# Expert routing with one-hot products of nine columns, and gathered rows scaled on the ScalarE before a plain transpose

## The chip, the core and the metric

One core of a Trainium2 chip runs one layer of a network. The metric is the device time of one launch, in microseconds (us), as the median of a few runs. TensorE (PE in the profile, with its weight loads as PEld) multiplies matrices, VectorE (DVE) and ScalarE (ACT) work on elements, GpSimd (POOL) issues the transfers whose addresses are read from a tile, and SyncE (SP) issues the others.

## What is computed

The layer is attention and a short convolution, followed by a mixture of 16 experts, in which each expert chooses 128 of the 1024 tokens. The change lies in the second part:

```python
def ec_moe(x_tok, w_router, w_gate, w_up, w_down):
    cap = CAP_FACTOR * t // N_EXPERTS            # 128 tokens for each expert
    aff = jax.nn.softmax(logits, axis=-1)
    g, idx = lax.top_k(jnp.swapaxes(aff, 1, 2), cap)
    xs = jax.vmap(lambda xt, ix: xt[ix])(x_tok, idx)
    hg = jnp.einsum('becd,edf->becf', xs, w_gate)
    hu = jnp.einsum('becd,edf->becf', xs, w_up)
    y = jnp.einsum('becf,efd->becd', jax.nn.silu(hg) * hu, w_down) * g[..., None]
    # y is added into the rows idx of a zero array
```

`x_tok` is the RMS norm of the stream `h`, scaled and shifted. The kernel gathers rows of `h` itself and multiplies each by its own norm factor (1 over its root mean square) afterwards.

## The kernel before

The experts run one after the other, in the loop that begins at L1550. An expert's weights are 24 pieces of 512 KB, `raw`, loaded by SP into a ring of 30 pages; SP waits for a page to come free before it issues the next load. Each piece is split into two parts: ACT writes the high part `whi` (L157), DVE subtracts it and writes the low part `wlo` (L158). There are four buffers of each (`NSP = 4`), so ACT can be at most four pieces ahead of PE. PE uses a piece in six matmuls of 512 columns, in three kinds in turn: `whi` with the high part of the activations (L162), `wlo` with it (L163), `whi` with their low part (L164). In the order of pieces an expert has 4 for `hg`, 4 for `hu`, 4 for the second half of `hg`, 4 for the second half of `hu`, and 8 for the output `pyy`. This text counts them 1 to 24.

What the next expert needs is made by `route(e + 1)`, called after the first `hg`:

- DVE compares positions with a row of numbers and gets eight one-hot matrices `oh` (L1460).
- 24 small bf16 matmuls (L1465) multiply them with `tokb` into `pi`, three columns: the token's index, its gate and its norm factor. Each of the three is kept in three bf16 parts, which is why there are 8 times 3 matmuls: the parts are added in PSUM.
- ACT turns column 0 into the integer `idx` (L1467), and POOL issues the gather `xs <- hS` (L1469).
- DVE copies `pi` to `slot` (L1472) and makes `dgx`, the identity times the norm factor (L1474).

`xsplit`, called after the second `hu`, multiplies the gathered rows with `dgx` (L1511), which transposes and scales them at once, into `ptt`. ACT applies the affine (`xsy`, L1513), and ACT and DVE split it (`xsh`, `xsl`). At an expert's end ACT scales `pyy` by the gate into `y` (L1604) and POOL adds `y` into `ffS` by an indirect transfer (L1605).

SP's order is written by hand. The order on the other engines in this stage is made by a scheduler when the program is built, and each engine then runs its instructions in that fixed order.

Of the kernel before, what the change touches and what calls it, by code (L numbers as in the profile page):

```python
# [10 lines left out]
F32 = mybir.dt.float32  # L11
# [3 lines left out]
AF = mybir.ActivationFunctionType  # L15
OP = mybir.AluOpType
AX = mybir.AxisListType
# [3 lines left out]
P = 128  # L21
# [5 lines left out]
E = 16  # L27
KT = 8
# [119 lines left out]
def build(tc, nc, I, out, dbg=None):  # L148
    V, S, G, PE, SY = nc.vector, nc.scalar, nc.gpsimd, nc.tensor, nc.sync
# [3 lines left out]
    def f(ap):  # L153
        return ap.bitcast(F32)

    def split(hi, lo, src, eng=V):
        i = S.activation(hi, src, AF.Copy)  # L157
        eng.tensor_sub(lo, src, f(hi))  # L158
        return i
# [7 lines left out]
    with es:  # L167
# [4 lines left out]
        sm = es.enter_context(tc.tile_pool(name="sm", bufs=4))  # L172
        dr = es.enter_context(tc.tile_pool(name="dr", bufs=1, space=DRAM))
        pgA = es.enter_context(tc.tile_pool(name="pgA", bufs=NPA))
        psB = es.enter_context(tc.tile_pool(name="psB", bufs=3, space=PSUM))

        def pool(stack, name, bufs=1, **kw):
            return stack.enter_context(tc.tile_pool(name=name, bufs=bufs, reuse_waits="tile", **kw))

        def page(p, name, dt=F32, shape=(P, D)):  # L180
            return p.tile(list(shape), dt, name=name, tag="pg")

        def bank(shape, name):
            return psB.tile(list(shape), F32, name=name, tag="b")
# [42 lines left out]
        def const(n, shape, dt=F32, eng=SY):  # L227
            t = cp.tile(shape, dt, name=n)
            eng.dma_start(out=t, in_=I[n])
            return t  # L230
# [173 lines left out]
        for i, o in enumerate(ORDER.split()):  # L404
            if i == NL0:
                npm = const("npm", [P, KT])
                ident = const("ident", [P, P])
# [100 lines left out]
        for i in range(10):  # L508
# [6 lines left out]
            for j in range(2):  # L515
                S.dma_start(out=vS[:, :, j, i, :].rearrange("h p e -> p h e"),
                            in_=f(hl[:, j, :]).rearrange("p (h e) -> p h e", h=H))
# [632 lines left out]
        def transp(c, qt, g):  # L1150
            par = qt % 2
            k0, n = GRP[g]
            if par == 0:
                at[g] = (atp.tile([P, n, 2 * P], F32R, name=f"ath{g}"), atp.tile([P, n, 2 * P], F32R, name=f"atl{g}"))
            hi, lo = at[g]
            ps = psE[0].tile([P, 4, P], F32, name="ptr", tag="acc") if psE else bank([P, 4, P], "ptr")
            for j in range(n):
                PE.transpose(out=ps[:, j, :], in_=c[1][0][:, (k0 + j) * P:(k0 + j + 1) * P], identity=ident)  # L1158
            sl = slice(par * P, par * P + P)
            return hi[:, :, sl], lo[:, :, sl], ps[:, :n, :]  # L1160
# [84 lines left out]
        for i, (h, qt) in enumerate(seq):  # L1245
            j = i + 2
# [14 lines left out]
            def score():  # L1261
                c = scores(qq[j], KK[seq[j][0]])
                cs.append(c)
                return c
# [8 lines left out]
            c = None  # L1273
            if SO[i // 16] == 0:
                if j < N:
                    c = score()
                x0 = transp(cs[i], qt, 0)
                x1 = transp(cs[i], qt, 1)
# [15 lines left out]
            else:  # L1294
# [4 lines left out]
                if j < N:  # L1299
                    c = score()  # L1300
# [56 lines left out]
        def eacc(name):  # L1357
            return psE[0].tile([P, 512], F32, name=name, tag="acc")
# [22 lines left out]
        x1 = pool(e6, "x1")  # L1381
        tokb = rq.tile([P, KT, E, 3, 3], BF, name="tokb")
# [60 lines left out]
        pp = bank([P, KT, 2 * E], "pp5")  # L1443
# [5 lines left out]
        for j in range(KT - 1):  # L1449
            n = KT - 1 - j  # L1450
            PE.matmul(pp[:, j + 1:KT, :], onesb, gf[:, j:j + 1, :].to_broadcast([P, n, 2 * E]), start=False,
                      stop=(j == KT - 2))
# [5 lines left out]
        def route(e):  # L1458
            oh = x1.tile([P, KT, P], BF, name="oh")
            V.tensor_tensor(out=oh, in0=late["iota"][:, None, :].to_broadcast([P, KT, P]),  # L1460
                            in1=pos[:, :, e:e + 1].to_broadcast([P, KT, P]), op=OP.is_equal)
            pi = bank([P, 3], "pi")
            for j in range(KT):
                for k in range(3):
                    PE.matmul(pi, oh[:, j, :], tokb[:, j, e, k, :], start=(j + k == 0), stop=(j == KT - 1 and k == 2))  # L1465
            idx = sm.tile([P, 1], I32, name="idx")
            S.activation(idx, pi[:, 0:1], AF.Copy)  # L1467
            xs = x1.tile([P, D], F32, name="xs")
            G.indirect_dma_start(out=xs, out_offset=None, in_=hS[:, :],  # L1469
                                 in_offset=bass.IndirectOffsetOnAxis(ap=idx[:, :1], axis=0))  # L1470
            s = sm.tile([P, 3], F32, name="slot")
            V.tensor_copy(out=s, in_=pi)  # L1472
            dg = x1.tile([P, P], F32, name="dgx")
            V.tensor_scalar(dg, ident, s[:, 2:3], None, op0=OP.mult)  # L1474
            g = s[:, 1:2]
            return idx, g, xs, s, dg

        def tsplit(src, k0, hi, lo):
            pp = bank([P, 4, P], "ptt")
# [21 lines left out]
                hi, lo = w[kt // 2]  # L1501
                mm3(ps, xh_[:, kt, :], xl_[:, kt, :], hi[:, kt % 2, :], lo[:, kt % 2, :], kt == 0, kt == KT - 1)

        def xsplit(xs, dg, eng=V):

            hi, lo = x1.tile([P, KT, P], F32R, name="xsh"), x1.tile([P, KT, P], F32R, name="xsl")
            for k in range(0, KT, 4):
                pp = bank([P, 4, P], "ptt")
                y = x1.tile([P, 4, P], F32, name="xsy", bufs=2)
                for j in range(4):  # L1510
                    PE.matmul(pp[:, j, :], xs[:, (k + j) * P:(k + j + 1) * P], dg, start=True, stop=True)  # L1511
                for j in range(4):
                    S.activation(y[:, j, :], pp[:, j, :], AF.Identity, bias=mv[:, 1, k + j:k + j + 1],  # L1513
                                 scale=mv[:, 2, k + j:k + j + 1])
                split(hi[:, k:k + 4, :], lo[:, k:k + 4, :], y, eng)
            return hi, lo
# [22 lines left out]
        def glu(hg, hu):  # L1539
# [3 lines left out]
            return a  # L1543

        cur = route(0)
        first = chunk(0, 0)
        xh_, xl_ = xsplit(cur[2], cur[4], V)
        eD.close()
        e5.close()
        for e in range(E):  # L1550
            idx, g = cur[:2]
            ach, acl = x1.tile([P, KT, P], F32R, name="ach"), x1.tile([P, KT, P], F32R, name="acl")
            acts = []
            for fh in range(2):
                hg = eacc("hg")
                prod(hg, xh_, xl_, chunk(e, 2 * fh) if e or fh else first)
                if fh and e + 1 == E:
                    tcopy(acts[0], 0, ach)
                elif fh:
                    tsplit(acts[0], 0, ach, acl)  # L1560
                elif e + 1 < E:
                    nxt = route(e + 1)
                else:
                    bc["G2"] = page(pgA, "bcG2")
                    load_bc("G2")

                    ffg = page(pgA, "ffg")
                    G.indirect_dma_start(out=ffg, out_offset=None, in_=ffS[:, :],
                                         in_offset=bass.IndirectOffsetOnAxis(ap=idx[:, :1], axis=0))
                    for t in range(KT):  # L1570
                        fr.append(page(pgA, "ffr"))
                        G.dma_start(out=fr[t], in_=ffS[t * P:(t + 1) * P, :])
                hu = eacc("hu")
                prod(hu, xh_, xl_, chunk(e, 2 * fh + 1))
                acts.append(glu(hg, hu))
            if e + 1 < E:
                xh_, xl_ = xsplit(nxt[2], nxt[4])
            pys = [eacc("pyy") for _ in range(2)]
            if e + 1 == E:

                for i in range(KT):
                    if i == TSJ:
                        tcopy(acts[1], 4, ach)
                    if i % 2 == 0:
                        final(i // 2)
                    if not raws:
                        load_raw(pgX if (nraw[0] - NR0) % (NPA + NPX) < NPX else pgA)
                    raw = raws.popleft()
                    for dh in range(2):
                        PE.matmul(pys[dh], f(ach[:, i, :]), raw[:, dh, :], start=i == 0, stop=i == KT - 1)  # L1590
                continue
            for c in range(2):
                w = chunk(e, 4 + c)
                for j in range(4):
                    if c == 0 and j == TSJ:
                        tsplit(acts[1], 4, ach, acl)
                    hi, lo = w[j]
                    kt = 4 * c + j
                    for dh in range(2):
                        mm3(pys[dh], ach[:, kt, :], acl[:, kt, :], hi[:, dh, :], lo[:, dh, :], kt == 0, kt == KT - 1)  # L1600
            if e + 1 < E:
                y = x1.tile([P, D], F32, name="y")
                for dh in range(2):
                    S.activation(y[:, dh * 512:dh * 512 + 512], pys[dh], AF.Copy, scale=g[:, 0:1])  # L1604
                G.indirect_dma_start(out=ffS[:, :], out_offset=bass.IndirectOffsetOnAxis(ap=idx[:, :1], axis=0),  # L1605
                                     in_=y, in_offset=None, compute_op=OP.add)
                cur = nxt

        sl2 = sm.tile([P, 2], F32, name="ssl")
        for dh, sl in enumerate(halves):  # L1610
# [7 lines left out]
                             in_=ffg, in_offset=None)  # L1618
# [15 lines left out]
```

## Time and profile before

| what | value |
|---|---|
| median of 3 runs | 1348.53 us (1345.4 to 1351.03) |
| the profiled execution's own time | 1347.07 us |
| its span, first to last instruction | 1345.3 us |
| busy: PE, PEld | 92%, 75% of the span |
| busy: DVE, ACT | 80%, 59% |
| mean granted TensorE clock | 0.955 of full |
| the stage of the experts | about 735 to 1310 us |

A busy share is the time in which an engine executes something, over the span. It is a mean over stages with different limits, so the stage of the experts is read by itself further on.

### The profile page before, as it was taken

What the parts mean: (1) busy time and instruction counts of PE and PEld (TensorE: products, weight loads), DVE (VectorE), ACT (ScalarE), POOL (GpSimd) and SP (SyncE); (2) the same over time, 40 slices, a digit from 0 to 9 for tenths busy, and PEclk for the clock granted to TensorE, in tenths of its full rate; (3) what the DMA queues carried; (4) which work ended last, traced back from release to release, by engine and by line L of the source; (5) the groups of instructions that cost most, each with busy time, mean ns of one, the idle gap of its engine ahead of it and who ended that gap; (6) DMA issues with size and microseconds to landing.
All of it is one profiled execution on the core that took longest, in us unless ns stands there. A gap on an engine that the chain in (4) does not pass through costs nothing. (4 is left out here: it accounts for less than half of the span.)

```text
span 1345.3 us, 18451 instructions
## 1 busy us (share of the span) xinstructions
PE 1239.2 (92%) x6407; PEld 1009.8 (75%) x6407; DVE 1078.0 (80%) x1834; ACT 795.1 (59%) x1183; POOL 68.1 (5%) x64
## 2 busy tenths in 40 slices
PE   6999999999999799899863999999999999999993
PEld 2588887888888678677753888888888888877761
DVE  5972565979788857698867899999999999888865
ACT  5732112444344535454442988888888888887861
POOL 0000000000000000000000000000000000010022
PEclk8999999999999889899975999999999999999997
DMA  8449448355476963324197999999999999999497
GB/s 346 141 82 340 137 134 274 121 160 174 133 179 209 279 207 113 139 87 144 53 397 271 309 390 381 378 377 375 379 372 375 381 371 376 378 354 368 121 379 155
DMA packets 139053, 347.69 MB, mean 258 GB/s; under 512 B 16976, under 2 KB 59472, under 8 KB 138320
## 3 DMA queue, kind: packets, MB, share of 16 engines
q1 hardware_dynamic: 109760, 306.14, 63.9%
q0 software_dynamic: 7056, 25.69, 7.2%
q10 hardware_dynamic: 22144, 14.68, 3.8%
q8 instruction: 50, 0.82, 0.2%
q14 instruction: 43, 0.35, 0.1%
HBM read 297.17 MB, written 49.30 MB: 258 GB/s over the span
## 5 line engine op out<-in xcount | busy, mean ns | idle before, releaser
L158 DVE TENSOR_TENSOR wlo<-raw,whi 128x1024 fp32r<-128x1024 f32 x376 | 440.7, 1219 | 33.0 <-ACT whi L157 28.2
L157 ACT ACTIVATE whi<-raw 128x1024 fp32r<-128x1024 f32 x376 | 388.9, 1067 | 61.4 <-PE hu L164 27.9
L1131 ACT ACTIVATE e<-ps,nm 128x1280 f32<-128x1280 f32 x64 | 84.5, 1326 | 68.4 <-DVE nm L1127 52.8
L1127 DVE TENSOR_REDUCE nm<-ps 128x1 f32<-128x1280 f32 x64 | 92.5, 1482 | 17.5 <-PE ps L1118 17.4
L162 PE MATMUL hu<-whi,xsh 128*128 128x512 f32 x256 | 102.6, 401 | 1.6 <-ACT whi L157 1.6
L163 PE MATMUL hu<-wlo,xsh 128*128 128x512 f32 x256 | 101.8, 398 | 0.8 <-DVE wlo L158 0.8
L164 PE MATMUL hg<-whi,xsl 128*128 128x512 f32 x256 | 99.8, 390 | 1.1 <-DVE xsl L158 1.1
L163 PE MATMUL hg<-wlo,xsh 128*128 128x512 f32 x256 | 100.4, 392 | 0.0
L164 PE MATMUL hu<-whi,xsl 128*128 128x512 f32 x256 | 100.3, 392 | 0.0
L162 PE MATMUL hg<-whi,xsh 128*128 128x512 f32 x256 | 100.0, 390 | 0.0
L163 PE MATMUL pyy<-wlo,ach 128*128 128x512 f32 x240 | 94.9, 395 | 1.4 <-DVE wlo L158 0.9
L1118 PE MATMUL ps<-KK,q 128*128 128x512 f32 (+1 forms) x384 | 90.5, 382 | 6.1 <-ACT e L1131 3.6
L1163 ACT ACTIVATE ath<-ptr 128x512 fp32r<-128x512 f32 (+1 forms) x96 | 47.4, 525 | 80.9 <-PE ptr L1158 80.4
L162 PE MATMUL pyy<-whi,ach 128*128 128x512 f32 x240 | 94.1, 402 | 0.0
L164 PE MATMUL pyy<-whi,acl 128*128 128x512 f32 x240 | 93.9, 391 | 0.0
L1118 PEld LDWEIGHTS ps<-KK,q 128*128 128x128 f32 x384 | 64.8, 201 | 17.3 <-ACT e L1131 5.4
L671 PE MATMUL pf<-xh,wh 128*128 128x512 f32 x192 | 75.3, 392 | 1.7 <-DVE gc L689 1.7
L675 PE MATMUL pf<-xh,wl 128*128 128x512 f32 x192 | 75.9, 395 | 0.0
L673 PE MATMUL pf<-xl,wh 128*128 128x512 f32 x192 | 75.3, 392 | 0.0
L1166 DVE TENSOR_TENSOR atl<-ptr,ath 128x512 fp32r<-128x512 f32 (+1 forms) x96 | 55.5, 594 | 13.3 <-ACT ath L1163 13.0
L162 PEld LDWEIGHTS hu<-whi,xsh 128*128 128x128 f32 x256 | 48.4, 189 | 11.4 <-ACT whi L157 2.1
L163 PEld LDWEIGHTS hu<-wlo,xsh 128*128 128x128 f32 x256 | 48.6, 190 | 11.0 <-DVE wlo L158 1.8
(316 smaller groups left out, 2662.0 us busy)
## 6 DMA issues: line engine op xcount, KB each, us to landing
raw<-in_we SPq DMA_DIRECT2D x384, 512.0 KB, 9.5
wa<-in_wa SPq DMA_DIRECT2D x32, 512.0 KB, 5.8
wraw<-in_wF SPq DMA_DIRECT2D x20, 512.0 KB, 5.4
waw<-in_wa SPq DMA_DIRECT2D x16, 512.0 KB, 6.2
q<-qS SPq DMA_DIRECT2D x64, 128.0 KB, 4.8
mS<-hl SPq DMA_DIRECT2D x48, 128.0 KB, 4.7
vS<-hv ACTq DMA_DIRECT2D x20, 256.0 KB, 5.2
KK<-kS SPq DMA_DIRECT2D x16, 320.0 KB, 7.4
```

Of the source, the lines that this page charges most:

```text
L157: i = S.activation(hi, src, AF.Copy)
L158: eng.tensor_sub(lo, src, f(hi))
L162: PE.matmul(ps, wh, mh, start=first, stop=False)
L163: PE.matmul(ps, wh, ml, start=False, stop=False)
L164: PE.matmul(ps, wl, mh, start=False, stop=last)
L671: PE.matmul(ps, wh[:, kt, :], xh[kt][:, sl], start=first, stop=False)
L673: PE.matmul(ps, wh[:, kt, :], xl[kt][:, sl], start=False, stop=False)
L675: PE.matmul(ps, wl[:, kt, :], xh[kt][:, sl], start=False, stop=last)
L1118: PE.matmul(ps[:, m, k0:k0 + n], q[:, m, j, :], KK[:, m, k0:k0 + n], start=(j == 0), stop=(j == 1))
L1127: V.tensor_reduce(out=c[1][-1], in_=c[0][:, m, :], axis=AX.X, op=OP.max, negate=True)
L1131: S.activation(e, c[0][:, m, :], AF.Exp, bias=c[1][3 + m], accum_out=l[:, m:m + 1])
L1166: V.tensor_sub(x[1], x[2], f(x[0]))
```

## The change

The 24 small products become 8 of nine columns each, one for each block of 128 tokens; the three parts that PSUM used to add are added by a DVE reduction, which writes `slot`. `idx` is then a DVE copy from `slot` in place of an ACT instruction from `pi`. The matrix `dgx` goes. The gathered rows are scaled by an ACT instruction of 128x1024 (in place, except for the last expert), and transposed by PE against the plain identity.

```diff
-            pi = bank([P, 3], "pi")
+            pi = bank([P, 9], "pi")
             for j in range(KT):
-                for k in range(3):
-                    PE.matmul(pi, oh[:, j, :], tokb[:, j, e, k, :], start=(j + k == 0), stop=(j == KT - 1 and k == 2))
+                PE.matmul(pi, oh[:, j, :], tokb[:, j, e, :, :].rearrange("p k c -> p (k c)"), start=(j == 0),
+                          stop=(j == KT - 1))
+            s = sm.tile([P, 3], F32, name="slot")
+            V.tensor_reduce(out=s, in_=pi.rearrange("p (k c) -> p c k", c=3), axis=AX.X, op=OP.add)
             idx = sm.tile([P, 1], I32, name="idx")
-            S.activation(idx, pi[:, 0:1], AF.Copy)
+            V.tensor_copy(out=idx, in_=s[:, 0:1])
             xs = x1.tile([P, D], F32, name="xs")
             G.indirect_dma_start(out=xs, out_offset=None, in_=hS[:, :],
                                  in_offset=bass.IndirectOffsetOnAxis(ap=idx[:, :1], axis=0))
-            s = sm.tile([P, 3], F32, name="slot")
-            V.tensor_copy(out=s, in_=pi)
-            dg = x1.tile([P, P], F32, name="dgx")
-            V.tensor_scalar(dg, ident, s[:, 2:3], None, op0=OP.mult)
-            g = s[:, 1:2]
-            return idx, g, xs, s, dg
+
+            xn = xs if e + 1 < E else page(pgA, "xn")
+            S.activation(xn, xs, AF.Copy, scale=s[:, 2:3])
+            return idx, s[:, 1:2], xs, s, xn
...
-                    PE.matmul(pp[:, j, :], xs[:, (k + j) * P:(k + j + 1) * P], dg, start=True, stop=True)
+                    PE.transpose(out=pp[:, j, :], in_=xs[:, (k + j) * P:(k + j + 1) * P], identity=ident)
```

The scheduler moves things on three engines. On DVE, in each of the middle experts, the program before has this, from the split of the gathered rows on (`act` is the product of the two halves of the SwiGLU):

```order
L158 TENSOR_TENSOR xsl<-xsy,xsh 128x512
L158 TENSOR_TENSOR wlo<-raw,whi 128x1024 x11
L1460 TENSOR_TENSOR oh<-iota,pos 128x1024
L1472 COPY slot<-pi 128x3
L158 TENSOR_TENSOR wlo<-raw,whi 128x1024
L1474 TENSOR_SCALAR dgx<-ident,slot 128x128
```

The changed program has this at the same place:

```order
L158 TENSOR_TENSOR xsl<-xsy,xsh 128x512
L158 TENSOR_TENSOR wlo<-raw,whi 128x1024 x7
L1467 TENSOR_REDUCE slot<-pi 128x3
L1460 TENSOR_TENSOR oh<-iota,pos 128x1024
L158 TENSOR_TENSOR wlo<-raw,whi 128x1024
L1469 CAST idx<-slot 128x1
L158 TENSOR_TENSOR wlo<-raw,whi 128x1024 x6
L1542 TENSOR_TENSOR act<-act,hu 128x512
```

`slot` comes four pieces earlier, and `idx` follows it on DVE behind the next expert's `oh` and one more `wlo`: it stands right after the `wlo` of piece 4.

On ACT the program before has this from the output of the expert before on:

```order
L1604 ACTIVATE y<-pyy,slot 128x512 x2
L157 ACTIVATE whi<-raw 128x1024 x5
L1467 ACTIVATE idx<-pi 128x1
L1541 ACTIVATE act<-hg 128x512
L157 ACTIVATE whi<-raw 128x1024 x8
L157 ACTIVATE ach<-ptt 128x512
```

The changed program has this, here with the semaphores that each row waits for (DMASW is that of a POOL transfer, here the gather; DMAHW are those of the weight loads):

```order
L1604 ACTIVATE y<-pyy,slot 128x512 [waits PE_49] x2
L157 ACTIVATE whi<-raw 128x1024 [waits DMAHW6_49,DVE_49]
L157 ACTIVATE whi<-raw 128x1024 [waits DMAHW7_49,DVE_49,PE_49]
L157 ACTIVATE whi<-raw 128x1024 [waits DMAHW0_49,DVE_49,PE_49]
L157 ACTIVATE whi<-raw 128x1024 [waits DMAHW1_49,DVE_49,PE_49]
L157 ACTIVATE whi<-raw 128x1024 [waits DMAHW2_49,DVE_49,PE_49]
L1541 ACTIVATE act<-hg 128x512
L157 ACTIVATE whi<-raw 128x1024 [waits DMAHW3_49,DVE_49,PE_49]
L1475 ACTIVATE xs<-xs,slot 128x1024 [waits DMASW3_49]
L157 ACTIVATE whi<-raw 128x1024 [waits DMAHW4_49,DVE_49,PE_49]
L157 ACTIVATE whi<-raw 128x1024 [waits DMAHW5_49,DVE_49,PE_49]
```

`idx` is gone from ACT, and the scaling stands between the `whi` of piece 9 and that of piece 10. So five pieces lie between `idx` on DVE and the scaling on ACT. That holds for 9 of the gathers (for the experts of index 2 to 10); for the next two it is four pieces, and for the last three it is three. On PE the small products of the middle experts stand before among the matmuls of the same expert, between the first `hg` and `hu`; in the changed program they stand 26 matmuls into `pyy` of the expert before.

## Rows read from the trace of the kernel before

**Rows 1.** Windows of the experts' stage: busy us of each engine, granted clock, DMA.

```profile
core 0: us, PE busy (x) PEld busy (x) DVE busy (x) ACT busy (x) POOL busy (x), PEclk, DMA share, GB/s
735.00:1180.00 445.00, 445.00 (x2354) 369.97 (x2355) 404.88 (x405) 388.73 (x502) 39.39 (x25) 1.00 1.01 372
```

**Rows 2.** Waits of PE, 730 to 1310 us, the first of four: us, times, longest.

```profile
PE hu L162 <- ACT whi L157: 1.6, 1, 1.6
...
```

**Rows 3.** Timeline of PE: start us, us, what.

```profile
847.92 0.76 PE L1465 MATMUL pi<-tokb,oh 128*128 128x3 bf16 x24
848.54 0.47 PE L162 MATMUL hu<-whi,xsh 128*128 128x512 f32 x1
...
865.44 1.95 PE L1511 MATMUL ptt<-dgx,xs 128*128 128x128 f32 x16
867.14 0.48 PE L162 MATMUL pyy<-whi,ach 128*128 128x512 f32 x1
...
868.61 0.60 PE L1481 MATMUL ptt<-ident,act 128*128 128x128 f32 x4
868.96 0.48 PE L162 MATMUL pyy<-whi,ach 128*128 128x512 f32 x1
```

**Rows 4.** Timeline of ACT in the same expert, with idle before and its releaser.

```profile
849.08 0.15 ACT L1467 ACTIVATE idx<-pi 128x1 int32<-128x1 f32 x1
850.21 1.06 ACT L157 ACTIVATE whi<-raw 128x1024 fp32r<-128x1024 f32 x1 [0.49 <-PE hu L164]
851.57 1.06 ACT L157 ACTIVATE whi<-raw 128x1024 fp32r<-128x1024 f32 x1 [0.30 <-PE hu L164]
```

**Rows 5.** Timeline of DVE in the same expert.

```profile
835.83 8.04 DVE L158 TENSOR_TENSOR wlo<-raw,whi 128x1024 fp32r<-128x1024 f32 x7 [0.18 <-ACT whi L157]
849.05 1.22 DVE L1460 TENSOR_TENSOR oh<-iota,pos 128x1024 bf16<-128x1024 f32 x1
850.19 0.15 DVE L1472 COPY slot<-pi 128x3 f32<-128x3 f32 x1
```

**Rows 6.** Timeline of POOL in the same expert.

```profile
843.80 1.59 POOL L1605 DMA_INDIRECT ffS<-y,idx  x1 [28.86 <-ACT y L1604]
849.50 1.63 POOL L1469 DMA_INDIRECT xs<-hS,idx  x1 [4.10 <-ACT idx L1467]
```

**Rows 7.** DMA issues from 740 to 1180 us, median us from issue to landing.

```profile
ffS<-y,idx POOLq DMA_INDIRECT x12, 10.1
xs<-hS,idx POOLq DMA_INDIRECT x12, 8.2
```

**Rows 8.** Tile `xs`, 690 us to the end, all 16 gathers: time to landing.

```profile
DMA to landing us min/median/max: 5.2/8.2/11.8
```

**Rows 9.** Groups of ACT and DVE, 740 to 1180 us: busy us, mean ns | idle before.

```profile
L157 ACT ACTIVATE whi<-raw 128x1024 fp32r<-128x1024 f32 x293 | 304.8, 1068 | 54.2 <-PE hu L164 26.1 <-PE hg L164 19.7 <-PE pyy L164 6.0
L1604 ACT ACTIVATE y<-pyy,slot 128x512 f32<-128x512 f32 x24 | 15.0, 675 | 0.0
L158 DVE TENSOR_TENSOR wlo<-raw,whi 128x1024 fp32r<-128x1024 f32 x292 | 342.3, 1219 | 16.1 <-ACT whi L157 11.4
```

**Rows 10.** Timelines of ACT and PE in the last expert, 1286 to 1292 us.

```profile
1287.18 0.60 ACT L1541 ACTIVATE act<-hg 128x512 f32<-128x512 f32 x1 [3.18 <-PE hg L164]
...
1288.77 0.50 PE L162 MATMUL hu<-whi,xsh 128*128 128x512 f32 x1 [1.63 <-ACT whi L157]
1290.03 0.79 PE L163 MATMUL hu<-wlo,xsh 128*128 128x512 f32 x1 [0.76 <-DVE wlo L158]
```

**Rows 11.** Window of that place: the columns of rows 1.

```profile
1290.00:1293.40 3.40, 3.37 (x8) 2.68 (x9) 3.38 (x3) 2.39 (x3) 0.69 (x1) 0.53 1.02 374
```

**Rows 12.** DMA rate in 40 slices, 740 to 1180 us.

```profile
GB/s 276 379 269 356 412 406 325 414 404 339 379 410 352 367 410 356 351 414 403 330 406 407 335 368 410 359 354 409 406 324 415 403 325 385 409 360 359 411 366 347
```

**Rows 13.** Timelines of PE and ACT at the first gather.

```profile
728.66 3.76 PE L1511 MATMUL ptt<-dgx,xs 128*128 128x128 f32 x16 [5.83 <-DMA xs<-hS,idx]
730.74 1.51 ACT L1513 ACTIVATE xsy<-ptt,mv 128x128 f32<-128x128 f32 x4 [7.70 <-PE ptt L1511]
```

More of the change, by code (lines that the diff above doesn't have):

```diff
@@ L1502, in prod, with xsplit @@
                 mm3(ps, xh_[:, kt, :], xl_[:, kt, :], hi[:, kt % 2, :], lo[:, kt % 2, :], kt == 0, kt == KT - 1)
-        def xsplit(xs, dg, eng=V):
+        def xsplit(xs, eng=V):
             hi, lo = x1.tile([P, KT, P], F32R, name="xsh"), x1.tile([P, KT, P], F32R, name="xsl")
@@ L1546, in build @@
         first = chunk(0, 0)
-        xh_, xl_ = xsplit(cur[2], cur[4], V)
+        xh_, xl_ = xsplit(cur[4], V)
         eD.close()
@@ L1576, in build @@
             if e + 1 < E:
-                xh_, xl_ = xsplit(nxt[2], nxt[4])
+                xh_, xl_ = xsplit(nxt[4])
             pys = [eacc("pyy") for _ in range(2)]
```

## The prediction

> **What bounds the kernel now.** I read the windows first. From 735 to 1180 us PE is busy in all of the 445 us at the full granted clock, DVE in 404.88 and ACT in 388.73 [rows 1]. The waits of PE agree: from 730 to 1310 us they are of four kinds, the longest single one 1.6 us [rows 2]. So PE sets the pace of the middle experts, and DVE, at 91%, is close behind. The transfers are not the bound: SP's weight loads wait for free pages, and the rate reaches 415 GB/s in single slices against a mean of 372 [rows 1, 12]. Then I went through one expert engine by engine in the timelines [rows 3 to 6]. Two consecutive `whi`, each waiting for PE to free a buffer, start 1.36 us apart: that is PE's time for one piece of weights [rows 4]. ACT is thus held back to four pieces ahead of PE; DVE runs seven `wlo` on end behind ACT [rows 5]. An engine in front of PE that stops for long therefore starves PE after some three pieces, about 4 us. [...]
>
> **What the change takes from PE.** The 24 small products hold PE from 847.92 to 848.54, 0.62 us; eight cost a third, 0.21, if each matmul costs the same with nine columns as with three [rows 3]. The 16 passes of the product with `dgx` (two records for each matmul) hold it from 865.44 to 867.14, 1.70 us. Four plain transposes hold it from 868.61 to 868.96, 0.35, so eight cost 0.70 [rows 3]. That is 0.41 + 1.00 = 1.41 us for an expert, all on the path as long as PE is the bound. For 15 experts: **-21.0 us**.
>
> **DVE and ACT by volume.** DVE loses `dgx` and a copy and gets a reduction and a copy of one column; nothing of weight. ACT gets 1.07 us for each expert, by the `whi` of the same shape [rows 9], less the 0.15 of `idx` [rows 4]. By two `y` of half the size it would be 1.35 [rows 9]. ACT's 388.73 of 445 us [rows 1] become about 0.9 of the time: by volume this is hidden behind PE.
>
> **The wait that the change adds.** The scaling stands in ACT's order between the `whi` of pieces 9 and 10, and it waits for the gather. Behind it are queued all further `whi`, and behind them `wlo` and PE. The gather can't be issued before `idx`, which now stands on DVE. I put it together on the clock of the expert in the rows:
>
> - The seven `wlo` end at 835.83 + 8.04 = 843.87 [rows 5]. The chain from `ptt` over `xsy` to these is held by ACT and DVE, so I leave it where it is.
> - Reduction 0.2 (the copy of the same three columns takes 0.15; the reduction of nine is not in this trace), `oh` 1.22, `wlo` 1.22, `idx` 0.15: 846.7 [rows 5, 9].
> - POOL starts 0.27 us after `idx` is done, as before [rows 4, 6]: 846.9. It is free then, its scatter having taken from 843.80 to 845.39 [rows 6].
> - The gather takes 8.2 us from issue to landing [rows 7]: 855.1.
> - Scaling 1.07, `whi` of piece 10 1.06, its `wlo` 1.22: **858.5** [rows 4, 9].
>
> PE needs that `wlo` for the second matmul of piece 10. Before, `hu` begins at 848.54; five pieces and one matmul later (5 x 1.36 + 0.23, and 0.08 for the slower first step) it is 855.65. In the changed kernel PE is there 1.41 us sooner: **854.2**. So PE is late by 4.3 us, three times the 1.41 that it gains (each PE wait then is a little under that, since the first `oh` of the list already holds up `wlo` by some tenths). The case in [rows 10] supports the step: 3.18 us of waiting on ACT cost PE 2.4.
>
> By the order rows this holds for 9 gathers. Where only four pieces lie between `idx` and the scaling, PE is one piece less far, and the loss is 4.3 + 1.36 = 5.7 us (2 gathers); with three pieces 7.0 us (3 gathers). Sum: 9 x 4.3 + 2 x 5.7 + 3 x 7.0 = **+71.1 us**.
>
> **The clock.** A hole of about 4 us with one matmul inside is longer than the 1.63 + 0.76 after which the clock fell [rows 10, 11]. I expect one such stretch behind each of the 14 stalls: 3.4 us at about half speed is 1.7 us of lost work each, **+23.8 us**. The bounds are 0 and twice that.
>
> **The start.** The first `idx` now stands behind an `oh` (1.2 us) and the scaling adds 1.07, while the products and transposes at the start, at the low clock, lose about 1.5 (8 of the 16 passes took the 2.1 us from 728.66 to 730.74 [rows 13], four transposes should take half): +0.8. The second gather, whose scaling stands only two pieces behind its `idx`, costs 0 to 2 us: +1.
>
> **Sum.** 1347.1 - 21.0 + 71.1 + 23.8 + 1.8 = 1422.8, **1423 us**. The sum starts from the profiled execution's own 1347.07 us; the runs' median is 1.5 us above that, well inside their spread.
>
> **The bounds.** What matters most is the landing of the gather. The lowest of the 16 is 5.2 us and the highest 11.8 [rows 8]. I take the median, because 12 gathers in the middle experts share it, right behind the same scatter [rows 7]. With 5.2 the loss of 9 gathers is 1.3 us, of the others 2.7 and 4.0: 29 us, and holes of that size may leave the clock alone: 1358. With 10.1, what the scatter in the same queue takes [rows 7], it is 1.9 us more for each of 14: 1450. With 11.8, 1473. The scaling at 1.35 adds 4 us. A slower PE also asks for fewer weights in the same time, which should shorten the landing a little, not lengthen it.
>
> [...]
>
> **Rivals.**
>
> 1. *ACT doesn't get to the scaling before the gather has landed: faster.* For this the landing may take 3.9 us at most (8.2 - 4.3); up to about 5.3 the middle experts still gain something with the full clock. It leaves -21.0 + 1.8, so **1328 us**. For it: the volume of work on ACT and DVE fits. Against it: the lowest of 16 gathers took 5.2 us [rows 8]. Chance 0.06. [...]
> 2. *The gather lands in about 5.2 us* because PE's stalls thin out the weight loads: **1358 us**. For it: the lowest of the 16 took that [rows 8]. Against it: the loads in flight when the gather is issued come from the pieces just before, which DVE frees at full speed. Chance 0.10, of which 0.03 come out within 0.5% of before.
> 3. *The gain on PE is eaten by something else and nothing is lost*, for instance by the DMA engines, which already are busy at a share of 1.01 [rows 1]: **1347 us**. Against it: the rates above 400 GB/s [rows 12]; 372 would have to become 387. Chance 0.03.
> 4. *The same stalls, but worse*, with late gathers or two low stretches of the clock for each: **1470 us**. Chance 0.05.
>
> **How the numbers follow.** My forecast, the stall at the scaling with or without the clock, has the remaining 0.76, at 1385 to 1460. The range that holds the time 8 times in 10 takes in rival 2 and ends below the worst of rival 4: **1360 to 1465 us**. Under 0.5%, about 7 us, this kernel's runs can't tell a change from none. Faster 0.06 (rival 1), same 0.06 (rival 3 and a part of 2), slower 0.88.
>
> **What would show it.** In the profile after, ACT should have a wait for the DMA of `xs` at the scaling, of some 4 us, in each middle expert, and longer in the last four or five. PE, which waits for nothing now, should wait for `whi` and `wlo` right behind it, in the second `hg`, 3 to 4 us each time, with a granted clock near 0.5 in the stretch after. `ptt` should have half its records, and `pi` a third. The time between two scatters on POOL should grow by 4 to 5 us. The prediction is wrong if the scaling's wait is short (the gather is early, rival 1 or 2), if PE's work was not what the gap contains (no idle time on PE, yet a longer period), or if the clock stays full, which alone makes it 1399.

## The result, and the profile after

The changed kernel takes **1487.50 us** (median of 4 runs, 1481.16 to 1491.47) against 1349.78 for the kernel before on the same chip (4 runs): ratio 1.102, interval 1.099 to 1.104. It is slower by 138 us; by the forecast of 1423 us it would have been 73. The profiled execution has a span of 1479.4 us at a mean granted clock of 0.924, where before had 1345.3 and 0.955.

The waits of ACT and of PE, 700 us to the end (us in total, times, longest), to set beside [rows 2]:

```profile
ACT xs L1475 <- DMA xs<-hS,idx: 142.6, 14, 30.1
ACT xn L1475 <- DMA xs<-hS,idx: 3.7, 1, 3.7
```

```profile
PE hg L162 <- ACT whi L157: 73.6, 11, 7.5
PE hu L162 <- ACT whi L157: 19.5, 6, 6.4
```

ACT waits at the scaling in 15 of the 16 gathers (`xn` is the tile that takes the last expert's scaled rows), and PE, which waited 1.6 us at most before, waits for ACT behind it. The longest wait, 30.1 us, belongs to the first gather, ahead of all experts. The other 14 are those of the forecast: nine of 8.8 to 9.7 us, 9.2 on average, then five of 3.7 to 8.4. This is the mechanism of the forecast at twice its size. One of the nine shows where, engine by engine: POOL, DVE, ACT and PE (start us, us, what, idle before and its releaser), answering to [rows 3 to 6]:

```profile
910.08 1.78 POOL L1605 DMA_INDIRECT ffS<-y,idx  x1 [36.89 <-ACT y L1604]
913.55 5.79 POOL L1471 DMA_INDIRECT xs<-hS,idx  x1 [1.69 <-PE hg L164]
```

```profile
910.39 1.21 DVE L1460 TENSOR_TENSOR oh<-iota,pos 128x1024 bf16<-128x1024 f32 x1
911.53 1.22 DVE L158 TENSOR_TENSOR wlo<-raw,whi 128x1024 fp32r<-128x1024 f32 x1
912.66 0.14 DVE L1469 CAST idx<-slot 128x1 int32<-128x1 f32 x1
912.73 5.76 DVE L158 TENSOR_TENSOR wlo<-raw,whi 128x1024 fp32r<-128x1024 f32 x5
928.05 1.22 DVE L158 TENSOR_TENSOR wlo<-raw,whi 128x1024 fp32r<-128x1024 f32 x1 [9.56 <-ACT whi L157]
```

```profile
915.83 1.05 ACT L157 ACTIVATE whi<-raw 128x1024 fp32r<-128x1024 f32 x1
925.92 1.15 ACT L1475 ACTIVATE xs<-xs,slot 128x1024 f32<-128x1024 f32 x1 [9.04 <-DMA xs<-hS,idx]
926.98 3.88 ACT L157 ACTIVATE whi<-raw 128x1024 fp32r<-128x1024 f32 x4
```

```profile
928.07 0.80 PE L162 MATMUL hg<-whi,xsh 128*128 128x512 f32 x1 [6.92 <-ACT whi L157]
929.33 0.79 PE L163 MATMUL hg<-wlo,xsh 128*128 128x512 f32 x1 [0.46 <-DVE wlo L158]
929.92 0.63 PE L164 MATMUL hg<-whi,xsl 128*128 128x512 f32 x1
...
933.32 0.39 PE L163 MATMUL hg<-wlo,xsh 128*128 128x512 f32 x1
933.55 0.39 PE L164 MATMUL hg<-whi,xsl 128*128 128x512 f32 x1
```

`idx` is ready at 912.80 and POOL begins the gather 0.75 us later. The gather instruction itself then takes 5.79 us, where it took 1.63 before [rows 6]. ACT gets the rows 12.4 us after POOL began, and PE stands for 6.92 and 0.46 us. Note where POOL's instruction ends: 913.55 + 5.79 = 919.34, which is 0.85 us after the five `wlo` on DVE end (912.73 + 5.76 = 918.49). The landing time of all 16 gathers, against [rows 8], and the DMA issues from 740 to 1300 us, against [rows 7]:

```profile
DMA to landing us min/median/max: 4.4/12.2/13.0
```

```profile
ffS<-y,idx POOLq DMA_INDIRECT x12, 10.0
xs<-hS,idx POOLq DMA_INDIRECT x12, 12.4
```

The scatter is as quick as it was; the gather is later by 4.2 us, which is POOL's 5.79 - 1.63. But the median stands for nine gathers only, those of the experts of index 2 to 10: POOL takes 5.8 us in each, and they land after 12.2 to 13.0 us. The last five stand in another order of DVE; POOL takes 1.2 to 3.5 us there, and they land after 6.3 to 10.5. Two of the five begin 2.0 us behind `idx`, because the scatter now stands just ahead of them on POOL:

```profile
1185.86 1.59 POOL L1605 DMA_INDIRECT ffS<-y,idx  x1 [39.64 <-DVE idx L1469]
1187.75 2.03 POOL L1471 DMA_INDIRECT xs<-hS,idx  x1 [0.30 <-PE hg L164]
...
1325.30 3.48 POOL L1471 DMA_INDIRECT xs<-hS,idx  x1 [40.21 <-PE pyy L163]
```

Last the windows around the stall (the columns of [rows 1]; the granted clock stands after the brackets of POOL):

```profile
922.00:924.00 2.00, 0.00 (x0) 0.00 (x0) 0.00 (x0) 0.00 (x0) 0.00 (x0) 1.00 1.03 422
928.00:930.00 2.00, 1.47 (x3) 0.87 (x4) 1.95 (x3) 2.00 (x4) 0.00 (x0) 0.50 0.01 4
932.00:934.00 2.00, 2.00 (x7) 1.55 (x6) 2.00 (x3) 0.94 (x2) 0.00 (x0) 0.68 0.88 240
936.00:938.00 2.00, 2.00 (x10) 1.60 (x10) 1.84 (x3) 2.00 (x4) 0.00 (x0) 1.00 0.99 375
```

The granted clock is still full in the hole, 1.00 from 922 to 924 us. Behind it, it is 0.50 from 928 to 930 us, 0.68 from 932 to 934 and 1.00 again from 936 to 938.

### The profile page after: what moved, and what is told of

The parts are those of the page before. It is cut to its first block, busy times and chain, and to the rows that moved or that the text cites. A ratio compares the mean times of both kernels' runs of the same rounds, so it can differ in the third digit from the quotient of the medians.

```text
span 1479.4 us, 17669 instructions
## 1 busy us (share of the span) xinstructions
PE 1259.1 (85%) x6023; PEld 1009.1 (68%) x6023; DVE 1076.6 (73%) x1834; ACT 805.3 (54%) x1183; POOL 109.2 (7%) x64
## 5 line engine op out<-in xcount | busy, mean ns | idle before, releaser
L157 ACT ACTIVATE whi<-raw 128x1024 fp32r<-128x1024 f32 x376 | 384.1, 1063 | 58.7 <-PE hg L164 29.5
L162 PE MATMUL hg<-whi,xsh 128*128 128x512 f32 x256 | 112.5, 440 | 75.0 <-ACT whi L157 73.6
L162 PEld LDWEIGHTS hg<-whi,xsh 128*128 128x128 f32 x256 | 54.5, 213 | 91.6 <-ACT whi L157 78.2
L163 PE MATMUL hg<-wlo,xsh 128*128 128x512 f32 x256 | 112.2, 438 | 4.5 <-DVE wlo L158 4.4
L164 PE MATMUL hg<-whi,xsl 128*128 128x512 f32 x256 | 108.5, 424 | 0.0
L163 PE MATMUL hu<-wlo,xsh 128*128 128x512 f32 x256 | 104.9, 410 | 2.4 <-DVE wlo L158 2.4
L1475 ACT ACTIVATE xs<-xs,slot 128x1024 f32<-128x1024 f32 x15 | 17.2, 1146 | 142.6 <-DMA xs<-hS,idx 142.6
L162 PE MATMUL pyy<-whi,ach 128*128 128x512 f32 x240 | 89.8, 405 | 1.2 <-ACT whi L157 1.2
L1471 POOL DMA_INDIRECT xs<-hS,idx x16 | 64.9, 4055 | 177.1 <-PE pyy L163 82.0
```

The source lines that it names most:

```text
L162: PE.matmul(ps, wh, mh, start=first, stop=False)
L163: PE.matmul(ps, wh, ml, start=False, stop=False)
L164: PE.matmul(ps, wl, mh, start=False, stop=last)
```

## The experiments

Theory: ACT's place of the scaling is too early for the gather, and that wait is the whole loss. Rival: the new parts (nine columns, reduction, transposes, ACT's work) cost something themselves.

**e1, late scaling.** The scaling is emitted ahead of `xsplit`, behind `whi` of piece 16 in place of 9 (`last` is ACT's silu of the second half; of `r`, the results of `route`, 2 is `xs`, 3 is `slot` and 4 the tile for the scaled rows).

```diff
-            S.activation(xn, xs, AF.Copy, scale=s[:, 2:3])
...
+                with tc.issue_after(last.ins):
+                    S.activation(r[4], r[2], AF.Copy, scale=r[3][:, 2:3])
```

> The changed kernel with the scaling emitted after the second SwiGLU activation, so that in ACT's order it stands behind the whi of piece 16 in place of piece 9 (twelve pieces behind idx, not five). Theory (the loss is ACT's wait for a gather that lands 12 us after its issue, in front of the whi): the gather is there when ACT arrives, ACT's wait at the scaling falls from 9 us to under 1.5, PE's waits nearly vanish and the 1.41 us of PE work that the change takes from each expert come back: 1330 us, between 1322 and 1340. Rival (the loss is the volume of work put on ACT and DVE, or GpSimd's long gathers themselves, wherever the scaling stands): 1400 or more.

Measured: 1354.16 us, ratio 1.0035 [1.0018, 1.0053]; all ratios are against the kernel before on the same chip. ACT's wait at the scaling is gone but for the first gather's, and with it 133 us. But the time is not under that of before.

**e2, no scaling** (the norm factors of the gathered rows are left out): the `S.activation` is deleted.

> The changed kernel without the scaling: the gathered rows are transposed as they are, so the tokens' norm factors are left out of the result. Theory: no instruction on ACT waits for the gather, so the whole loss goes: 1328 us (1320 to 1338), and GpSimd's gathers may still take 5.8 us each without any price. Rival (the loss sits in the nine-column products, the reduction or the late idx): well above 1350.

Measured: 1348.23, ratio 0.9993 [0.9974, 1.0013]. The wait is the whole loss. PE's saving is not in the time.

**e3, the products alone.** `dgx` and the product with it stay; `pi`, `slot` and `idx` are as in the change.

> Only the first half of the change: 8 products of nine columns, the reduction and idx on DVE; the product with the scaled identity stays. Theory: no wait on ACT, PE has 0.41 us less for each of 15 experts: 1343 us (1338 to 1347). GpSimd's gathers stand before a run of wlo on DVE here too; if that run is what lengthens them, they take 4 to 6 us, not 1.6. Rival (nine columns cost more than three, or idx on DVE delays something): 1350 or more.

Measured: 1349.42, ratio 1.0008 [0.9980, 1.0036]: no effect.

**e4, the scaling alone.** The 24 products and ACT's `idx` of before; scaling on ACT and transposes of the change.

> Only the second half: the old 24 products and idx on ACT, but the rows scaled on ACT and plainly transposed. idx stands behind the whi of piece 2 and the scaling behind that of piece 5, three pieces later. Theory: the same stall as in the changed kernel; with three pieces 7.0 us for PE and 1.7 for the clock, less 1.0 of PE work, for 14 experts: 1455 us with gathers of 8.2 us; 1500 to 1520 if GpSimd's gathers are long here too. If they are short here (1.6 us on GpSimd), the DVE copy that makes idx, or what stands behind it, is what lengthens them. Rival (the products cause the loss): under 1350.

Measured: 1422.09, ratio 1.0549 [1.0493, 1.0605]. The scaling costs, but half as much as in the change, and POOL's gathers are short here, 1.30 to 1.35 us in all but one. So the products, harmless alone, add some 63 us by the ratios when the scaling waits behind them: with them POOL's gather is long (5.8 us in nine gathers of the change). It is long in e3 too, 3.71 us in eleven experts, but nothing on ACT waits for it there.

**e5 to e8: what holds the gather, and how the loss follows ACT's place.** e5 casts the index on ACT (`S.activation(idx, s[:, 0:1], AF.Copy)`). e6 puts a one-operand instruction of DVE behind the cast:

```diff
-            V.tensor_copy(out=idx, in_=s[:, 0:1])
+            ii = V.tensor_copy(out=idx, in_=s[:, 0:1])
+            if e:
+                with tc.issue_after(ii.ins):
+                    V.tensor_reduce(out=sm.tile([P, 1], F32, name="gap"), in_=f(xh_), axis=AX.XY, op=OP.max)
```

e7 moves the scaling behind piece 12. e8 is e1 with the instruction of e6.

> The changed kernel, with the index cast on ACT instead of DVE (the 8 products, the reduction, the scaling and the transposes stay). Theory A: POOL's gather is long (5.79 us) because it is let in only where a gapless run of DVE instructions with two operands ends, and an index that DVE writes just ahead of such a run misses the boundary; an index from ACT arrives inside an instruction, and the gather ends 0.8 to 0.9 us after the end of that one, as it did in the kernel with the scaling alone (1.3 us): POOL's gather 1.2 to 2.2 us, landing 8.5 to 9.5 us instead of 12.3, ACT's wait at the scaling down from 10 us to 4 to 6, time 1395 to 1430 us. Rival B: the length belongs to the form of the products (nine columns, reduction): the gather stays at 5 to 7 us and the time at 1470 us or more.

> The changed kernel with one more DVE instruction behind the index cast: a maximum over xsh, one SBUF operand, 1.1 us by the oh of as many elements, whose result nobody reads. Theory A (only DVE instructions with two SBUF operands keep POOL's gather out): the gather ends inside this instruction or within 1 us behind it, in at most 2.2 us instead of 5.79; landing 8 to 9.5 us instead of 12.3; ACT's wait shorter by 3 to 4 us at each of 14 scalings, time 1415 to 1440 us. Rival B (any run of DVE instructions without a gap holds the gather, whatever its operands, or the length is not DVE's doing): the gather takes 6.5 to 8 us and the time is 1487 us or up to 15 us more.

> The changed kernel with the scaling three pieces later in ACT's order (behind whi of piece 12 instead of 9; the kernel with late scaling has it behind 16). Theory A (the loss is what ACT's place lacks against the landing): three pieces of hu and hg are 3 x 1.76 us of PE, so ACT's wait falls from 10 us to about 5 per expert, or 6 if the gather grows to the 6.9 us that it took with late scaling; time 1395 to 1415 us. Rival B (a stall anywhere ahead of the transposes costs the same, since PE's order is filled just in time): 1470 us or more. Rival C (the stock of ready pieces covers 5 us): 1350 to 1365 us.

> Late scaling (behind whi of piece 16) together with the one-operand DVE instruction behind the index cast; the scheduler then keeps the even order of 24 pieces per expert up to the last but two, where late scaling alone went over to the interleaved order some four experts earlier. Theory A (the late order ate PE's saving): the scatters stand 35.2 to 35.4 us apart to the end, and the time is 1333 to 1343 us, under the kernel before. Rival B (the late experts are slower by another limit, the transfers or DVE): from 1050 us on they stand 37 to 38 us apart as with late scaling alone, and the time is 1350 to 1358 us. On the gather: 2.2 us or less by the theory that only two-operand DVE instructions hold it, 7 us or more otherwise.

e5: 1478.79, ratio 1.1002 [1.0968, 1.1035]. Theory A was wrong in the part on ACT: the gather took 5.97 us in eight of the experts, again to the end of DVE's run (912.50 + 5.97 = 918.47; DVE's run ends at 917.62). Which engine writes `idx` doesn't matter for the length. It does for the start: POOL begins 0.3 to 0.4 us after an `idx` from ACT, as it did before, and mostly 0.7 to 0.8 after one from DVE. POOL and DVE of e5:

```profile
912.50 5.97 POOL L1471 DMA_INDIRECT xs<-hS,idx  x1 [0.30 <-ACT idx L1469]
...
911.86 5.76 DVE L158 TENSOR_TENSOR wlo<-raw,whi 128x1024 fp32r<-128x1024 f32 x5
```

e6: 1444.99, ratio 1.0767 [1.0722, 1.0811], a little over the expected range. One more DVE instruction makes the kernel some 34 us faster by the ratios. POOL and DVE of e6:

```profile
906.27 0.98 POOL L1474 DMA_INDIRECT xs<-hS,idx  x1 [1.68 <-PE hg L164]
...
905.46 1.21 DVE L1472 TENSOR_REDUCE gap<-xsh 128x1 f32<-128x1024 f32 x1
906.58 4.62 DVE L158 TENSOR_TENSOR wlo<-raw,whi 128x1024 fp32r<-128x1024 f32 x4
```

The gather is through in 0.98 us beside the reduction, its landing takes 8.9 us, and ACT's wait at the scaling is 79.2 us in 12, 6.6 each. So of the 4.8 us that POOL saves, 3.5 reach the landing.

e7: 1412.09, ratio 1.0503 [1.0463, 1.0543], as theory A expected: ACT waits 60.1 us in 11, of which nine are 5.9 to 7.0, 6.4 on average. A piece holds PE for 1.36 us [rows 4], not for the 1.76 of the expectation, and POOL's gather takes 6.92 us here, 1.1 more. So the 9.2 us of the change should become 9.2 + 1.1 - 3 x 1.36 = 6.2. The loss follows the distance between the two places.

e8: 1347.88, ratio 1.0026 [1.0003, 1.0048]. The gather takes 0.98 us, but the scatters are 36.0 us apart, not 35.2: 1.2 us more on DVE slows each expert by 0.8, and PE waits 0.7 us for `wlo` in each, where e1 has 0.2. DVE is that close behind PE. The scatters stay so up to 1175 us, where e1 has 38 to 40 us from 1058 on.

**e9, e10: which DVE instruction lets POOL in.** e9 is e6 with `tensor_tensor(gap, f(xh_), f(xl_), max)` in the same place: two SBUF operands. e10 has a reduction of `ident` (0.28 us) behind the first `wlo` after the cast.

> The control to the kernel with the extra reduction: in the same place of the same order stands an instruction of DVE of about the same length (1.2 us) that reads two SBUF operands (a maximum of xsh and xsl). Theory A (two SBUF operands keep POOL's gather out, a gapless run of them to its end): the gather is held over this instruction and the run of wlo behind it, 6.5 to 7.2 us instead of the 0.97 us that it took beside the reduction, landing 12.5 to 13.5 us, time 1485 to 1510 us. Rival B (the shape of the order or the delay of 1.2 us is what helped, not the operands): the gather takes 2.2 us or less and the time is 1440 to 1455 us.

> The changed kernel with a short one-operand instruction of DVE (a maximum over ident, 128 x 128, 0.2 to 0.3 us) behind the first wlo after the index cast, where the kernel before had its slot copy and dgx. Theory A: the gather, which starts 0.75 us after the cast, is held to the end of that wlo (0.38 us) and let in at the short instruction: 1.2 to 1.3 us; landing 9 to 9.5 us, ACT's wait down by 3 us or more from 10 us, time 1440 to 1455 us. Rival B (0.2 us is too short, or the operands are not what counts): the gather takes about 6 us and the time is 1485 to 1492 us.

e9: 1487.45, ratio 1.1039 [1.1013, 1.1064]. e10: 1455.67, ratio 1.0817 [1.0790, 1.0844]. POOL and DVE of e9, then of e10:

```profile
920.61 5.79 POOL L1474 DMA_INDIRECT xs<-hS,idx  x1 [1.68 <-PE hg L164]
...
919.78 1.22 DVE L1472 TENSOR_TENSOR gap<-xsh,xsl 128x1024 bf16<-128x1024 f32 x1
920.91 4.63 DVE L158 TENSOR_TENSOR wlo<-raw,whi 128x1024 fp32r<-128x1024 f32 x4
```

```profile
904.63 1.25 POOL L1473 DMA_INDIRECT xs<-hS,idx  x1 [1.69 <-PE hg L166]
...
903.81 1.22 DVE L160 TENSOR_TENSOR wlo<-raw,whi 128x1024 fp32r<-128x1024 f32 x1
904.94 0.28 DVE L1500 TENSOR_REDUCE gap<-ident 128x1 f32<-128x128 f32 x1
```

With two operands the added instruction helps nothing: the gather ends 0.86 us after the whole run. With one operand 0.28 us are enough. This settles it for the delay, the engine of `idx` and the length: none of them is the cause. What is left is the number of SBUF operands, or that e9's instruction writes 1024 columns where the reductions write one. A gather in a late expert of e5 speaks for the operands. It began beside `acl`, which writes 512 columns from one operand in SBUF and one in PSUM, and it was through in 0.93 us:

```profile
1181.79 0.93 POOL L1471 DMA_INDIRECT xs<-hS,idx  x1 [33.25 <-PE pyy L164]
...
1181.52 0.68 DVE L158 TENSOR_TENSOR acl<-ptt,ach 128x512 fp32r<-128x512 f32 x1
```

In the kernel before the place was there by chance: `slot`, a copy out of PSUM, stood right behind `oh` [rows 5].

**e11 to e18: where PE's saving goes.** In e1 and e2 the early experts take 35.2 us from scatter to scatter (36.15 before), but from 1055 us on they take 37.8 to 40.0, but for one of 35.0: the scheduler goes over to another order there, in which PE's, ACT's and DVE's pieces of work are interleaved, as it does in the kernel before from 1169 us on. e11 holds the small products in their early place on PE; e12 adds the short instruction of e10 to it. e13 to e15 fix all of PE's order and the place of `oh` on DVE (e13 late scaling, e14 no scaling, e15 the kernel before). e16 to e18 do the same three with ACT and DVE fixed too. e14 and e17 leave the norm factors of the gathered rows out, as e2 does. All is done by edges of this kind (`hm` lists matmuls of the products, `l` is the `whi` of piece 8 or 16, `m` a `wlo`; e16 calls `route` ahead of the first `hg`, where the same matmul is `hm[-10]`):

```diff
+            with tc.issue_after(hm[-18].ins) if e else ExitStack():
                 for j in range(KT):
                     PE.matmul(pi, oh[:, j, :], tokb[:, j, e, :, :].rearrange("p k c -> p (k c)"), start=(j == 0),
...
+            with tc.issue_after(l.ins):
+                lasts[1] = S.activation(a, hg, AF.Silu)
+            with tc.issue_after(m.ins) if m else ExitStack():
+                V.tensor_mul(a, a, hu)
```

> Late scaling (behind whi of piece 16), with the one-hot products of the next expert held on PE behind the sixteenth last product of the rows before them, so that slot and oh keep their place of the early experts up to the tenth, and one a little later from there to the end, in place of the interleaved order. Theory A (the interleaved order ate PE's saving): scatters 35.2 us apart to about 1175 us, and the time is 1328 to 1342 us. Rival B (the late experts are limited by something else): 37 to 39 us apart from 1060 us on, and 1350 to 1356 us, as with late scaling alone.

> The kernel of late scaling and even order, with the short one-operand instruction of DVE besides, so that POOL's gather lands 4 us earlier. Theory A (with 10 us of cover nothing waits for the gather): the gather takes 1.2 to 1.3 us instead of 6.9 us, and the time is that of the late scaling in even order alone, within 4 us; 1328 to 1342 us if the even order gives PE's saving back, the best of all kernels here. Rival B (DVE is a second bound, so that even 0.25 us per expert shows): 4 us or more above the kernel without the short instruction.

> Late scaling, with the order fixed in all experts as it is in the early ones: the one-hot products behind matmul 25 of the 48 of the rows before them, the transposes behind the last matmul that stands ahead of them in the code, and oh behind the third wlo of an expert. Theory A (PE's saving of 0.92 us per expert in the early experts is real and the interleaved late order, chosen by the scheduler, takes it back): scatters 35.2 to 35.3 us apart to the fourteenth, which is 6 us under the kernel before at the ninth and 10 us more in the six behind it, against 3 us lost ahead of the first: 1328 to 1338 us, ratio 0.988 to 0.994, the only kernel of all that beats both. Rival B (transfers or DVE limit the late experts): 37 us or more apart from 1060 us on, 1348 to 1356 us.

> The same fixed order without the scaling (the norm factors of the gathered rows are left out of the result). Theory A: scatters 35.2 us apart to the end, 1325 to 1335 us; the difference to the kernel with late scaling in fixed order is what the late scaling still costs, 0 to 4 us. Rival B as there: 1343 to 1352 us.

> The kernel before with the same kind of edges, so that its last experts keep the order of its early ones too (one-hot products behind the first eight pairs of hg, as they stand there). By the order alone, without the change: scatters 36.1 to 36.2 us apart to the end instead of 38.4, 38.4 and 36.6 for the last three, 5 us: 1338 to 1344 us. If the late order costs nothing by itself: 1345 to 1350 us.

> Late scaling, with the order of the early experts fixed to the end on PE, ACT and DVE (silu of hg behind whi 8 and 16, the split of the first half's activations behind whi 16, that of the gathered rows behind whi 20, the product with hu behind wlo 10 and 19, slot behind wlo 3). Fixing PE's order alone left 37.7 us per expert from the tenth on, with ACT standing 1.7 us at silu, 2.1 at ach and 1.8 at xsy in each. Theory A (those three places of ACT take back PE's saving): scatters 35.2 to 35.5 us apart to the fourteenth and 1328 to 1338 us. Rival B (a limit that no order lifts, in transfers or in the rate of all three engines): 37 us or more apart from 1060 us on, 1346 to 1354 us.

> The same without the scaling (norm factors left out of the result). Theory A: 35.2 to 35.4 us apart to the end, 1325 to 1335 us. Rival B: as with late scaling, 1345 to 1352 us.

> The kernel before with its own early order fixed to the end on PE, ACT and DVE. Theory A: scatters 36.1 to 36.2 us apart to the fourteenth (before: 38.4, 38.4 and 36.6 for the last three), 1338 to 1344 us; so that of 15 us that the kernel with late scaling in full order is expected to stand below the kernel before, some 5 are the order's and 10 the change's. Rival B: 1345 to 1350 us.

| kernel | us | ratio, interval | scatters of the late experts apart, us |
|---|---|---|---|
| e11 | 1348.61 | 1.0031 [1.0008, 1.0054] | 38.3 to 40.6 |
| e12 | 1352.76 | 1.0042 [1.0020, 1.0063] | 39.0 to 41.1 |
| e13 | 1348.58 | 1.0003 [0.9982, 1.0024] | 37.2 to 38.7 |
| e14 | 1348.90 | 1.0010 [0.9992, 1.0028] | 37.9 to 38.8 |
| e15 | 1348.57 | 1.0005 [0.9984, 1.0025] | 37.2 to 39.1 |
| e16 | 1339.42 | 0.9930 [0.9904, 0.9957] | 36.1, the last three 35.2 to 35.5 |
| e17 | 1326.05 | 0.9852 [0.9828, 0.9876] | 35.2 |
| e18 | 1336.16 | 0.9916 [0.9890, 0.9941] | 36.1 |

e11 left the last experts interleaved in another way and tells nothing on the order; its expectation failed. e12 has short gathers (1.22 us) and nothing from them: its early experts take 35.2 us like those of e11, where the gather takes 6.9. Its time is 4.1 us above that of e11, just over the bound between the two theories, with intervals that overlap; that stays undecided. e13 to e15 refuted theory A as it stood: with PE's order fixed the late experts are as slow. But ACT shows why. An early and a late expert of e14 on ACT, both with PE's order fixed:

```profile
921.52 0.58 ACT L1549 ACTIVATE act<-hg 128x512 f32<-128x512 f32 x1
932.41 0.58 ACT L160 ACTIVATE ach<-ptt 128x512 fp32r<-128x512 f32 x1
938.33 1.84 ACT L1521 ACTIVATE xsy<-ptt,mv 128x128 f32<-128x128 f32 x5
...
1138.10 0.60 ACT L1549 ACTIVATE act<-hg 128x512 f32<-128x512 f32 x1 [1.66 <-PE hg L169]
1150.33 0.60 ACT L160 ACTIVATE ach<-ptt 128x512 fp32r<-128x512 f32 x1 [2.10 <-PE ptt L1487]
1156.96 1.85 ACT L1521 ACTIVATE xsy<-ptt,mv 128x128 f32<-128x128 f32 x5 [1.76 <-PE ptt L1519]
```

In ACT's own order these three stand two `whi` earlier in the late experts, so it waits 5.5 us for PE in each, ahead of `whi` that PE needs. PE in turn waits for `whi` and `wlo`, 10.2 us in all from 1100 to 1285 us, some 2 us for an expert that is 3.6 us longer. The wait has the same form as that of the scaling. e16 to e18 bear it out: with ACT and DVE fixed too, all are faster than the kernel before, by 0.7 to 1.5%. Whether ACT's order alone would do, no run shows, since DVE's is fixed with it. In e17 the first and the fifteenth scatter are these, 14 x 35.2 us apart:

```profile
772.81 1.79 POOL L1626 DMA_INDIRECT ffS<-y,idx  x1 [36.98 <-ACT y L1625]
...
1265.90 1.73 POOL L1626 DMA_INDIRECT ffS<-y,idx  x1 [31.27 <-DMA raw<-in_we]
```

e16 is above its expected range by 1 us, through the place of one product: the edge holds the product with `hu` behind `wlo` 19 at the earliest, the scheduler put it behind `wlo` 20 in eleven experts, and PE waits for it (waits of PE, 780 to 1300 us):

```profile
PE ptt L1490 <- DVE act L1563: 11.0, 11, 1.0
```

Those experts take 36.06 us, the last ones, where it stands behind `wlo` 19, 35.2. Without that it would be about 1339 - 11 x 0.87 = 1330, an estimate that no run here tested.

So e16 beats both kernels, but the order alone (e18) does as well without the change. The change's part on PE is worth e18 - e17 = 10 us when the scaling is left out, and as it stands the change costs 138.

## Why the prediction was wrong in size

- **The step that failed: "The gather takes 8.2 us from issue to landing [rows 7]: 855.1".** In nine gathers it measured 12.2 to 13.0, because POOL's own instruction took 5.8 us in place of 1.63. "POOL starts 0.27 us after `idx` is done" measured 0.75. Together that is 4.8 us for each of the nine, 43 us. In the other five, which stand in another order, the landing took 6.3 to 10.5, and with the late starts they add 10. So this step is 53 of the 58 us that lie between the sum, 1422.8, and the profiled execution, 1481.16; the smaller errors below nearly cancel. The prediction's own bound for a landing of 11.8 us was 1473. (Its bound for 5.2 us adds up to 1357, not 1358, which changes nothing.) I took the median of before as a property of the transfer; it held a wait of POOL that was short only because of what stood next on DVE. e6, e9 and e10 show this, and so do [rows 5, 6]: `oh` ends at 850.27, and POOL's gather 0.86 us behind it.
- **The mechanism held.** ACT waits at the scaling, PE right behind it, in the second `hg`; e2 shows that nothing else costs, and e1 that it is the wait: ACT's own work costs 6 us at most, e1 against e2. Rivals 1 and 2 are out, since the gathers came later, not sooner, and rival 3, by which nothing is lost, is out by the time. Rival 4, "worse, with late gathers" (1470), was the nearest, and by its cause the right one.
- **PE's stall**: 6.92 + 0.46 us instead of 4.3, the excess from the same step. The distance between scatters grew by 9.3 us over the first eight (36.15 to 45.5 on average), not by 4 to 5. Over the last three it grew by 7.2 to 7.5, which is the 7.0 + 1.7 - 1.41 of the forecast for three pieces. That is luck: those gathers didn't land as forecast, and in the kernel before these experts already took 36.6 to 38.4, in another order.
- **The clock**: about as forecast in the expert shown. From 929.92 to 933.32 matmuls start 0.425 us apart, 0.23 after that: 8 x 0.195 = 1.6 us, forecast 1.7, seen in the rows at 0.50 and 0.68.
- **PE's saving of 1.41 us** was 0.91 (36.13 to 35.22 on average, e18 against e17). The transposes came out nearly as worked out: 1.70 to 0.79. Eight products take 0.21 us in e3, as worked out, and its early experts stand 35.78 us apart, 0.36 less than before. But where the whole change puts them, in `pyy`, they hold PE for 0.56 us, with a wait of 0.20 for the `wlo` behind them (e17, timeline of PE):

```profile
906.67 0.36 PE L1471 MATMUL pi<-tokb,oh 128*128 128x9 bf16 x8
907.23 0.50 PE L168 MATMUL pyy<-wlo,ach 128*128 128x512 f32 x1 [0.20 <-DVE wlo L161]
```

In its last five experts e17's products take 0.22 us again, but the scatters stay 35.2 us apart, so the price lies in the place and not in the products.

- **DVE and ACT by volume** were hidden, as said, but with less room on DVE than "nothing of weight" suggests: in e8 1.2 us more cost 0.8.
- **The scaling** took 1.15 us (1.07 forecast), the reduction 0.16 (0.2).

## What to carry to other kernels

ACT's scaling, which waits for a transfer, was priced here by the distance between its place and the landing: 9.2 us of waiting in a middle expert, 6.4 three pieces later (e7), 0.9 in all from 740 to 1300 us behind piece 16 (e1). Everything queued behind it paid. So move such an instruction behind work that doesn't need it (here 133 us) before counting what it computes. The duration of POOL's gather in the old profile included what DVE was doing beside it (1.63 us there, 5.79 in the change, 0.98 in e6): look at what stands next on DVE, before taking its median over to a new order. And PE's saving showed in the time only where the fixed order of the other engines let it run (ratio 1.0010 in e14, 0.9852 in e17): check late stages for waits of the same form.

## What was not expected of the hardware

POOL's gather waited for DVE. From 745 us on I compared 280 gathers of the 20 kernels with DVE's instructions. All of the 250 that began inside a DVE instruction with two SBUF operands ended 0.80 to 0.88 us after the end of one of these. The 30 that began beside an idle DVE or one with a single SBUF operand took 0.93 to 0.98 us. Of the 250, 66 had only that one instruction to wait for; 131 were held to the end of a gapless run of two to six; 53 got in at a boundary inside a run, as in the kernel with the scaling alone (the run goes on to 903.53). None was held past a gap of DVE, or past an instruction with one SBUF operand (12 times it was one of 512 columns). From e4:

```profile
900.76 1.35 POOL L1469 DMA_INDIRECT xs<-hS,idx  x1 [38.56 <-ACT idx L1467]
...
895.49 8.04 DVE L158 TENSOR_TENSOR wlo<-raw,whi 128x1024 fp32r<-128x1024 f32 x7 [0.18 <-ACT whi L157]
```

What lets these in is open; the engine of `idx` doesn't tell them apart.

Side by side: POOL's gather took 0.98 us beside one operand (e6), 5.79 beside two with a run behind them (e9), and up to 7.12 where a run of six `wlo` held it through (e3: it began at 1175.29 and ended 0.86 us behind the run).
